# Second input split in groups of four blocks, ScalarE's dependent steps one product later, a fourth raw weight buffer

## The chip, the cores and the metric

The kernel runs on one core of one Trainium2 chip. The time is device microseconds of one execution; the median of three runs before the change is 1909.51 us (1908.23 to 1911.74). The engines are TensorE (PE; PEld are its weight loads), VectorE (DVE), ScalarE (ACT), GpSimd (POOL) and SyncE (SP), which issues the weight loads from memory.

## The reference

One step of a decoder layer on 264 tokens (256 of a prompt and 8 single ones), in fp32:

```python
h = h + 0.5 * swiglu(rmsnorm(h, g1), w1_gate, w1_up, w1_down)      # 2048 -> 5504 -> 2048
mix, states... = mixing_block(rmsnorm(h, gm), w_in, ...)           # mLSTM heads | gated convolution
h = h + mix
h = h + 0.5 * swiglu(rmsnorm(h, g2), w2_gate, w2_up, w2_down)
y = rmsnorm(h, g_final)

def swiglu(x, wg, wu, wd):
    return (jax.nn.silu(x @ wg) * (x @ wu)) @ wd
```

All weights are read once from memory (some 350 MB).

## The kernel before

**Split products.** Every fp32 operand is split into two fp16 parts: `high` (L249, ScalarE) rounds it, `low` (L257, VectorE) takes what is left. A product is the sum of high x high, high x low and low x high, so `three` (L384) issues three matmuls of 264 columns for each 128 x 128 block of weights. Activations lie transposed: 16 blocks of 128 channels x 264 tokens (`h[kb]`).

**Weights.** `plan` lists the weight tiles in the order of use. `fetch` (L263) takes the next: it issues its load on SyncE's queue (L284, L288, L292) into a raw fp32 buffer `wraw` of [128, 16, 128] (three of them), has ScalarE write the high part into `w` (four of them), and puts the low part into `held`; `release` (L327) issues VectorE's low part. About three products' tiles are under way ahead of TensorE (`room`, `AHEAD`). `wraw` comes free when its low part is done.

**Order of the work.** It is written out by hand. `tick` counts products (a half step in the middle of each), and `at(n, f)` issues `f` when the count is n further on. Each engine executes what was issued to it in order.

**A feed-forward layer** (`ffn`, L879) has two halves: gate and up products for 22 (21 in the second) blocks of 128 hidden channels, then 16 down products over these. A plain gate/up block `j` (`block`, L942) is two products of 48 matmuls; ScalarE takes the SiLU of the gate (L950, or L960 where the input is not yet scaled), VectorE multiplies by the up product (L899 or L897), and `activated` (L895) has ScalarE and VectorE split the result into `act[j]`.

**Pairs.** Blocks in `GU_SEVEN` (and some pairs of down blocks, `DOWN_SEVEN`) go through `product_pair` (L448): gate and up together, with high x high done plainly (L474) and the corrections by seven instead of eight block products on 132 columns each (L457, L458). For that VectorE forms sums of weights (`weight_sums`, L360 to L364) and sums of the input (`token_sums`, L446), and after it `join` (L503) puts the three banks together: a copy on ScalarE (L511), then `rest` on VectorE (L514 to L521). `by_seven` (L927) issues `rest` and, right behind it, ScalarE's SiLU (L933) one product later, and `activated` another half pair on.

**Second split of the input.** The first products of a layer run on the input without the norm's factor, since that factor `r` is not known yet; their results are multiplied by `r` (L957, L963). Meanwhile `renew` (L808) splits the input again, with gain and factor: for each of 16 blocks VectorE multiplies (L820), ScalarE takes the high part (`r`, L249), VectorE the low part (L257), two blocks every half product. `swap` makes the products use it from block 5 (first layer) or 3 (second) on; later `form` makes its token sums for the pairs.

**Range sums.** `watch` (L650) sums the absolute values of some columns of a result, on ScalarE (L658) in the feed-forward layers. The sums go into a test at the end of the kernel, on which a second pass in another number format depends. In a down product VectorE adds the result to `h` (L1020), and then the range sum of the same bank is issued.

**The mixing block** (`mix`, L1156) between the layers uses single buffers of the pool `tmp`, among them `wide` (L1359), which the tests use too.

Of the kernel before, what the change touches and what calls it, by code (L numbers as in the profile page):

```python
# [8 lines left out]
F32 = mybir.dt.float32  # L9
# [8 lines left out]
SEQ = 256  # L18
# [10 lines left out]
WK = 8  # L29
# [22 lines left out]
def spread(b0, b1, n):  # L52
# [1 line left out]


GU_SEVEN = {
    "1": spread(7, 21, 9) + spread(22, NFB - 1, 13), "2": spread(4, 21, 10) + spread(22, NFB - 1, 13),
}
DOWN_SEVEN = {
    ("1", 0): (1, 3, 4, 6, 7), ("1", 1): (1, 3, 4, 6),  # L60
# [112 lines left out]
def step(ctx: ExitStack, tc: tile.TileContext, a: dict, shared, bad=None):  # L173
# [89 lines left out]
    def fetch():  # L263

        if not plan:
            return
        key, src, n, m, several, sub = plan.pop(0)
        if half_size and key == "four":
            raw, parts = small()
        elif half_size and sub == 1:  # L270
            raw, parts = (t[:, WK:] for t in pair)
        elif half_size:
            raw = wpool.tile([128, WIDE, 128], F32, tag="wraw", name="wraw", bufs=3)
            parts = wpool.tile([128, WIDE, 2, 128], PART, tag="w", name="w", bufs=4)
# [25 lines left out]
        lows = []  # L300
        for src, h_, l_ in pairs:
            high(h_, src, sw)
            lows.append((l_, src, h_, sw))
        release()
        held.append((lows, (key, parts[:, :, 0], parts[:, :, 1], n, size(key, sub)), parts))
        if not lag[0]:
            release()


    held, lag, pair = [], [False], []  # L310

    def size(key, sub):
        return 0 if key == "four" else 2 if half_size and sub is None else 1
# [361 lines left out]

    def watch_tokens(z, j):

        sq = tmp.tile([128, 2, T], BF16, tag="yc", name="tokens", bufs=2)
        nc.scalar.activation(sq, z, AF.Square)

        def rest():
            ps = bank()[:, :T]
            for g in range(2):
                nc.tensor.matmul(ps, onesb, sq[:, g], start=(g == 0), stop=(g == 1))
            for i, op in enumerate((ALU.min, ALU.add)):
                nc.vector.tensor_reduce(
                    downs[:, i, j : j + 1], ps, axis=mybir.AxisListType.X, op=op
                )

        at(2, rest)  # L690
# [24 lines left out]
    def judge(x, bounds):  # L715

        n = x.shape[-1]
        ok = tmp.tile([128, 2 * SEQ], F32, tag="wide", name="ok", bufs=1)[:, :n]
        nc.vector.tensor_scalar(ok, x, bounds[0], None, op0=ALU.is_ge)
        nc.vector.scalar_tensor_tensor(  # L720
            ok, x, bounds[1], ok, op0=ALU.is_le, op1=ALU.mult
# [48 lines left out]
    class Norm:  # L770
# [34 lines left out]
            token_sums(t, self.groups[g])  # L805
            self.forms += [t[:, :, i] for i in range(4)]

        def renew(self, *blocks):  # L808

            for kb in blocks:  # L810
                g, i = kb // WK, kb % WK
                if kb == 0:
                    self.new = []
                if i == 0:
                    self.new.append(
                        self.fpool.tile([128, WK, 2, T], PART, tag=f"f{g}", name=f"r{g}")
                    )
                t, x = t264("sq"), self.new[g][:, i]
                gain = whole[:, self.col + kb : self.col + kb + 1]
                nc.vector.scalar_tensor_tensor(t, h[kb], gain, self.r, op0=ALU.mult, op1=ALU.mult)  # L820
                split(x, t, 1.0)

        def swap(self):
            self.groups, self.scaled = self.new, True
# [54 lines left out]
    def ffn(layer, norm, done, start=None, end=None):  # L879
        with ExitStack() as stack:  # L880
# [14 lines left out]
            def activated(j, i, zu, sg, src=None):  # L895
                if src is None:
                    nc.vector.tensor_tensor(zu, zu, sg, op=ALU.mult)  # L897
                else:
                    nc.vector.scalar_tensor_tensor(  # L899
                        zu, src, unit, sg, op0=ALU.mult, op1=ALU.mult  # L900
                    )
                g = i // WK
                if i % WK == 0:
                    groups[g] = apool.tile(
                        [128, min(WK, len(HALVES[0]) - i), 2, T], PART, tag=f"a{g}", name=f"a{g}"
                    )
                act[j] = t = groups[g][:, i % WK]
                high(t[:, 0, :], zu, sa[layer])
                rest = t[:, 1, :], zu, t[:, 0, :], sa[layer]
                if lag[0] and j < blocks[-1] - 2:  # L910
                    at(1.5, low, *rest)
                else:
                    low(*rest)
                n = len(blocks) // 2 * 2
                if half_size and i in (WK - 1, 2 * WK - 1, n - 1):
                    at(2, act_form, g, groups[g][:, : min(WK, n - WK * g)])

            groups, act_forms = {}, {}

# [6 lines left out]

            def by_seven(j, i):  # L927
                z, rest = join(product_pair((layer, "gu", j), norm.x, norm.forms, range(KB)))
                sg = t264("tb")

                def halves():
                    rest()
                    nc.scalar.activation(sg, z[:, 0], AF.Silu, scale=unit)  # L933

                at(1, halves)
                at(2, activated, j, i, z[:, 1], sg, z[:, 1])

            if half_size:
                spool[0] = stack.enter_context(tc.tile_pool(name=f"seven_{norm.tag}", bufs=1))
            for half, blocks in enumerate(HALVES):  # L940
                act = {}
                def block(i, j):  # L942
# [5 lines left out]
                    if norm.scaled:  # L948
                        sg = t264("tb")
                        nc.scalar.activation(sg, pg, AF.Silu, scale=unit)  # L950
                        watch(pg, scalar=True)
                        pu = gate_up(j, "u")
                        activated(j, i, t264("tc"), sg, pu)
                        watch(pu, scalar=True)
                        return
                    zg = t264("ta")
                    nc.vector.tensor_tensor(zg, pg, norm.r, op=ALU.mult)  # L957
                    watch(pg, scalar=True)
                    sg = t264("tb")
                    nc.scalar.activation(sg, zg, AF.Silu)  # L960
                    pu = gate_up(j, "u")
                    zu = t264("tc")
                    nc.vector.tensor_tensor(zu, pu, norm.r, op=ALU.mult)  # L963
                    activated(j, i, zu, sg)
                    watch(pu, scalar=True)

                for i, j in enumerate(blocks):
                    if half_size and j == (5 if start is not None else 3):
                        norm.swap()
                    if j in sevens:  # L970
                        by_seven(j, i)
# [6 lines left out]
                        for which in "gu":  # L978
                            early[2, which] = product((layer, which, 2), norm.x, range(KB))
                    if half_size and j == (3 if start is not None else 1):  # L980
                        for n in range(WK):
                            at(1 + n / 2, norm.renew, 2 * n, 2 * n + 1)
                        for g in range(2):
                            at(6 + g + (start is not None), norm.form, g)
                    lag[0] = half_size and j >= (3 if start is not None else 1)
                    if (j, "g") in early and not first:

# [17 lines left out]
                for db in range(0, KB - apart, 2):  # L1005
# [5 lines left out]
                    for i in (db, db + 1):  # L1011
                        final = half_size and i == KB - 1 and half == 1
                        if final:
# [3 lines left out]
                            (layer, "d", half, i), act, list(blocks),  # L1017
                            final=final,
                        )
                        nc.vector.scalar_tensor_tensor(  # L1020
                            h[i], ps, scale, h[i], op0=ALU.mult, op1=ALU.add
                        )
                        if half == 1:
                            done(i)
                        watch(ps, scalar=True)
                lag[0] = False
                release()
                if apart:
                    keys = [(layer, "d", half, db) for db in range(KB - apart, KB)]
                    end(keys, act, list(blocks), scale)  # L1030
# [90 lines left out]
    def judge_late():  # L1121

        late = stat[:, early[0] : len(stats)]
        n = len(stats) - early[0]
        ok = tmp.tile([128, 2, NSTAT], F32, tag="wide", name="ok", bufs=1)[:, :, :n]
        nc.vector.tensor_scalar(ok[:, 0], late, SUMS[0], None, op0=ALU.is_ge)
        count = const.tile([128, 1], F32, name="count")
        nc.vector.scalar_tensor_tensor(
# [27 lines left out]
def mix(tc, a, nm, n2, h, e):  # L1156
# [4 lines left out]
    product, split, rsqrt, column_sums, t264 = (  # L1161
        e["product"], e["split"], e["rsqrt"], e["column_sums"], e["t264"])
# [14 lines left out]
    for cb in range(8):  # L1177
        x3[8 + cb] = keep.tile([128, 2, T], PART, tag=f"yb{cb}", name=f"yb{cb}")
    ha = [keep.tile([128, 2, T], F32, tag=f"ha{i}", name=f"ha{i}") for i in range(NH)]

    inner = ExitStack()
    mp = inner.enter_context(tc.tile_pool(name="mixp", bufs=1))
# [125 lines left out]
    class Head:  # L1308
# [46 lines left out]

        def load_decays(self):
            if e["half_size"]:
                self.bc = tmp.tile([128, 2, SEQ], F32, tag="wide", name="bc", bufs=1)
            else:  # L1359
                self.bc = mp.tile([128, 2, SEQ], F32, tag="bc", name="bc", bufs=1)  # L1360
            queue.dma_start(self.bc, drows[self.hd].partition_broadcast(128))
# [480 lines left out]
```

## Time and profile before

| | |
|---|---|
| median of the runs | 1909.51 us |
| the profiled execution | 1917.14 us, its span 1915.4 us |
| mean granted TensorE clock | 0.978 |
| busy: TensorE / VectorE / ScalarE / GpSimd | 94% / 82% / 46% / 8% |
| read from memory | 366.72 MB, 198 GB/s with the writes over the span |

Rows of groups read: line, engine, operation, output<-inputs by the program's names, shapes, count | busy us, mean ns of one | idle time of the engine just before them and what ended it. Rows of waits: the engine, what it was to issue and its line <- whom it waited for: us in total, times, longest. Rows of the timeline: start us, duration us, engine, line, operation; in brackets the idle time before and what ended it. The granted clock is a share of full speed.

### The profile page before, as it was taken

Reading aid. Unit: us, or ns where it says so; the run is one execution under the profiler, and the core shown is the slowest. Engines: PE = TensorE matmul, PEld = TensorE weight load, DVE = VectorE, ACT = ScalarE, POOL = GpSimd, SP = SyncE. Lnnn points to the kernel's source line nnn. Section 1 sums busy time; section 2 is a strip of 40 time slices with the busy share of each in tenths; the row PEclk is TensorE's granted clock in tenths of the full one; section 3 lists DMA queues with packets and bytes.
Section 4 is the critical chain, followed back from the end, with each engine's and each line's share of the span. In section 5 each row is a group of like instructions: output and inputs, shape, how many; then the busy total and the mean of one; then the engine's idle time right before and its main releaser. Section 6 shows DMA issues by size and latency. Waiting matters only on the chain. (4 is left out here: it accounts for less than half of the span.)

```text
span 1915.4 us, 44686 instructions
## 1 busy us (share of the span) xinstructions
PE 1809.5 (94%) x19512; PEld 1605.0 (84%) x19512; DVE 1574.6 (82%) x2207; ACT 878.9 (46%) x1325; POOL 144.8 (8%) x200
## 2 busy tenths in 40 slices
PE   9699999999999989999999999799999999998996
PEld 7489889889898877888888888599989889897886
DVE  7688988898989788788888765789887898989775
ACT  7444443334344435376666644344443344443333
POOL 1000000000000122222120121000000000000021
PEclk9799999999999999999999999799999999999999
DMA  8255555565555556788886665365555565555543
GB/s 300 99 186 190 198 182 183 193 222 189 196 184 172 193 166 211 251 288 296 278 278 225 217 198 176 122 209 198 193 187 181 185 223 179 199 179 176 188 158 120
DMA packets 100684, 381.47 MB, mean 199 GB/s; under 512 B 10972, under 2 KB 20796, under 8 KB 90496
## 3 DMA queue, kind: packets, MB, share of 16 engines
q1 hardware_dynamic: 91280, 350.52, 54.4%
q0 software_dynamic: 8256, 27.57, 4.2%
q8 instruction: 154, 2.52, 0.5%
q10 hardware_dynamic: 944, 0.45, 0.1%
q14 instruction: 50, 0.41, 0.1%
HBM read 366.72 MB, written 11.78 MB: 198 GB/s over the span
## 5 line engine op out<-in xcount | busy, mean ns | idle before, releaser
L257 DVE SCALAR_TENSOR_TENSOR w<-wraw,w 128x2048 f16<-128x2048 f32 (+4 forms) x425 | 756.3, 1797 | 189.7 <-ACT w L249 189.4
L249 ACT ACTIVATE w<-wraw 128x2048 f16<-128x2048 f32 (+4 forms) x425 | 628.2, 1505 | 153.8 <-DMA wraw<-in_w1d 38.0
L387 PEld LDWEIGHTS <-w 128*128 128x128 f16 x3084 | 304.8, 99 | 110.7 <-DVE w L257 58.0
L386 PEld LDWEIGHTS <-w 128*128 128x128 f16 x3084 | 304.9, 99 | 75.6 <-issue 27.4
L385 PEld LDWEIGHTS <-w 128*128 128x128 f16 x3084 | 305.6, 99 | 51.9 <-ACT w L249 4.3
L387 PE MATMUL ps<-r,w 128*128 128x264 f16 x1056 | 299.3, 283 | 31.6 <-DVE w L257 31.6
L385 PE MATMUL ps<-r,w 128*128 128x264 f16 x1056 | 298.7, 283 | 23.3 <-ACT r L249 23.3
L386 PE MATMUL ps<-r,w 128*128 128x264 f16 x1056 | 298.4, 283 | 1.6 <-DVE r L257 0.2
L385 PE MATMUL ps<-xm,w 128*128 128x264 f16 x896 | 247.3, 276 | 0.0
L387 PE MATMUL ps<-xm,w 128*128 128x264 f16 x896 | 247.3, 276 | 0.0
L386 PE MATMUL ps<-xm,w 128*128 128x264 f16 x896 | 247.3, 276 | 0.0
L474 PEld LDWEIGHTS <-w 128*128 128x128 f16 x2174 | 208.3, 98 | 37.0 <-ACT w L249 8.2
L458 PEld LDWEIGHTS <-s 128*128 128x128 f16 x2160 | 209.6, 97 | 0.0
L457 PEld LDWEIGHTS <-s 128*128 128x128 f16 x2160 | 207.7, 96 | 0.5
L387 PE MATMUL ps<-a,w 128*128 128x264 f16 (+2 forms) x684 | 183.2, 274 | 17.2 <-DVE w L257 17.1
L385 PE MATMUL ps<-a,w 128*128 128x264 f16 (+2 forms) x684 | 183.3, 274 | 3.6 <-ACT w L249 3.6
L386 PE MATMUL ps<-a,w 128*128 128x264 f16 (+2 forms) x684 | 183.1, 273 | 0.0
L474 PE MATMUL ps<-r,w 128*128 128x264 f16 x1440 | 176.8, 276 | 3.4 <-ACT w L249 3.4
L360 DVE TENSOR_TENSOR s<-w 128x2048 f16<-128x2048 f16 (+1 forms) x141 | 166.3, 1180 | 7.5
L458 PEld LDWEIGHTS <-w 128*128 128x128 f16 x1634 | 159.2, 98 | 8.5 <-DVE w L257 6.4
L457 PEld LDWEIGHTS <-w 128*128 128x128 f16 x1634 | 159.1, 97 | 2.3
L457 PE MATMUL ps<-f,s 128*128 128x132 f16 x1080 | 133.7, 220 | 0.0
(284 smaller groups left out, 2657.5 us busy)
## 6 DMA issues: line engine op xcount, KB each, us to landing
wraw<-in_w2gu SPq DMA_DIRECT2D x86, 1024.0 KB, 5.1
wraw<-in_w1gu SPq DMA_DIRECT2D x82, 1024.0 KB, 5.4
wraw<-in_win SPq DMA_DIRECT2D x112, 512.0 KB, 5.7
wraw<-in_w1d SPq DMA_DIRECT2D x18, 1024.0 KB, 5.2
wraw<-in_wout SPq DMA_DIRECT2D x32, 512.0 KB, 4.8
wraw<-in_w2d SPq DMA_DIRECT2D x16, 1024.0 KB, 6.6
wraw<-in_w2d SPq DMA_DIRECT2D x22, 704.0 KB, 4.2
wraw<-in_w1d SPq DMA_DIRECT2D x20, 704.0 KB, 4.1
```

What stands on the lines that cost most here:

```text
L249: nc.scalar.activation(dst, src, AF.Copy, scale=scale)
L257: nc.vector.scalar_tensor_tensor(dst, src, scale, hi, op0=ALU.mult, op1=ALU.subtract)
L360: nc.vector.tensor_tensor(s[:, 0:2], bc, d_.unsqueeze(1).to_broadcast([128, 2, m, 2, 128]), op=ALU.add)
L385: nc.tensor.matmul(ps, wh, xk[:, 0, :], start=first, stop=False)
L386: nc.tensor.matmul(ps, wh, xk[:, 1, :], start=False, stop=False)
L387: nc.tensor.matmul(ps, wl, xk[:, 0, :], start=False, stop=last)
L457: nc.tensor.matmul(ps, w[0], x[:, 1], start=first, stop=False)
L458: nc.tensor.matmul(ps, w[1], x[:, 0], start=False, stop=last)
L474: nc.tensor.matmul(ps[:, :T], hi[:, i], xs[i][:, 0], start=(k0 + i == 0), stop=False)
```

## The change

- **Renewal.** `renew` takes four blocks in three steps half a product apart: VectorE's four products with gain and factor into an fp32 buffer `wide` (tag `g0`/`g1` of the layer's pool), one `high` over 4 x 264 elements on ScalarE, one subtraction over 4 x 264 on VectorE. The four groups start at 1, 1.5, 2.5 and 3 products. In the first layer the new input is used from block 6 on instead of 5, and the token sums come one step later.
- **ScalarE's steps.** In `by_seven` the SiLU is issued one tick behind `rest`, and the multiplication half a tick behind that. For all blocks on the renewed input but the last three of a half, `high` of the activation (`parted`) is issued one product after the multiplication, and its low part a product after that. The sums of activations for the down pairs start once a group is complete.
- **Range sums in front.** `watch` is issued before VectorE's reading of the same result.
- **A fourth raw buffer.** Every fourth tile of the feed-forward layers takes its `wraw` from the layer's own pool.
- **Fewer pairs.** Three gate/up blocks become plain: 8 and 12 in the first layer's halves (9 and 13 before), 10 and 12 in the second's (10 and 13).
- **Buffers.** `wide` of `tmp` goes: the tests use tag `ta`, the mixing block's `bc`, `zo`, `rs`, `yc` lie in its own pool.

```diff
-    "1": spread(7, 21, 9) + spread(22, NFB - 1, 13), "2": spread(4, 21, 10) + spread(22, NFB - 1, 13),
+    "1": spread(7, 21, 8) + spread(22, NFB - 1, 12), "2": spread(4, 21, 10) + spread(22, NFB - 1, 12),
...
+        elif half_size and spool[0] and key[0] in ("1", "2") and next(turn) % 4 == 3:
+            raw = spool[0].tile([128, WIDE, 128], F32, tag="wraw", name="wraw", bufs=1)
+            parts = wpool.tile([128, WIDE, 2, 128], PART, tag="w", name="w", bufs=4)
...
-        def renew(self, *blocks):
-            for kb in blocks:
...
-                t, x = t264("sq"), self.new[g][:, i]
-                gain = whole[:, self.col + kb : self.col + kb + 1]
-                nc.vector.scalar_tensor_tensor(t, h[kb], gain, self.r, op0=ALU.mult, op1=ALU.mult)
-                split(x, t, 1.0)
+        def renew(self, pool, k0, step):
+            g, i = k0 // WK, k0 % WK
+            if step == 0:
...
+                for k in range(4):
+                    gain = whole[:, self.col + k0 + k : self.col + k0 + k + 1]
+                    nc.vector.scalar_tensor_tensor(
+                        self.wide[g][:, i + k], h[k0 + k], gain, self.r, op0=ALU.mult,
+                        op1=ALU.mult,
+                    )
+                return
+            t, x = self.wide[g][:, i : i + 4], self.new[g][:, i : i + 4]
+            if step == 1:
+                high(x[:, :, 0], t, 1.0)
+            else:
+                nc.vector.tensor_tensor(x[:, :, 1], t, x[:, :, 0], op=ALU.subtract)
...
+                if src is None or j >= blocks[-1] - 2:
+                    parted(j, i, zu)
+                else:
+                    at(1.5, parted, j, i, zu)
+
+            def parted(j, i, zu):
...
                 high(t[:, 0, :], zu, sa[layer])
-                rest = t[:, 1, :], zu, t[:, 0, :], sa[layer]
+                rest = g, i, t[:, 1, :], zu, t[:, 0, :], sa[layer]
                 if lag[0] and j < blocks[-1] - 2:
-                    at(1.5, low, *rest)
+                    at(1.5, lower, *rest)
                 else:
-                    low(*rest)
+                    lower(*rest)
+
+            def lower(g, i, *rest):
+                low(*rest)
                 n = len(blocks) // 2 * 2
-                if half_size and i in (WK - 1, 2 * WK - 1, n - 1):
-                    at(2, act_form, g, groups[g][:, : min(WK, n - WK * g)])
+                count[g] += i < n
+                size = min(WK, n - WK * g)
+                if half_size and i < n and count[g] == size:
+                    at(1, act_form, g, groups[g][:, :size])
...
-                sg = t264("tb")
-                def halves():
-                    rest()
+                late = j >= blocks[-1] - 2
+                def gate():
+                    sg = t264("tb")
                     nc.scalar.activation(sg, z[:, 0], AF.Silu, scale=unit)
-                at(1, halves)
-                at(2, activated, j, i, z[:, 1], sg, z[:, 1])
+                    at(0.5, activated, j, i, z[:, 1], sg, z[:, 1])
+                at(1, rest)
+                at(1 if late else 2, gate)
...
                         pu = gate_up(j, "u")
+                        watch(pu, scalar=True)
                         activated(j, i, t264("tc"), sg, pu)
-                        watch(pu, scalar=True)
...
-                    if half_size and j == (5 if start is not None else 3):
+                    if half_size and j == (6 if start is not None else 3):
                         norm.swap()
...
-                        for n in range(WK):
-                            at(1 + n / 2, norm.renew, 2 * n, 2 * n + 1)
+                        for n, t in enumerate((1, 1.5, 2.5, 3)):
+                            for step in range(3):
+                                at(t + step / 2, norm.renew, spool[0], 4 * n, step)
                         for g in range(2):
-                            at(6 + g + (start is not None), norm.form, g)
+                            at(6 + g + 2 * (start is not None), norm.form, g)
...
+                        watch(ps, scalar=True)
                         nc.vector.scalar_tensor_tensor(
                             h[i], ps, scale, h[i], op0=ALU.mult, op1=ALU.add
                         )
                         if half == 1:
                             done(i)
-                        watch(ps, scalar=True)
...
-                self.bc = tmp.tile([128, 2, SEQ], F32, tag="wide", name="bc", bufs=1)
+                self.bc = keep.tile([128, 2, SEQ], F32, tag="bc", name="bc", bufs=1)
```

More of the change, by code (lines that the diff above doesn't have):

```diff
@@ L307, in fetch @@
             release()
-    held, lag, pair = [], [False], []
+    held, lag, pair, turn = [], [False], [], iter(range(10000))
     def size(key, sub):
@@ L676, in watch_tokens @@
     def watch_tokens(z, j):
-        sq = tmp.tile([128, 2, T], BF16, tag="yc", name="tokens", bufs=2)
+        sq = tmp.tile([128, 2, T], BF16, tag="ta", name="tokens", bufs=2)
         nc.scalar.activation(sq, z, AF.Square)
@@ L717, in judge @@
         n = x.shape[-1]
-        ok = tmp.tile([128, 2 * SEQ], F32, tag="wide", name="ok", bufs=1)[:, :n]
+        ok = t264("ta")[:, :n]
         nc.vector.tensor_scalar(ok, x, bounds[0], None, op0=ALU.is_ge)
@@ L806, in form @@
             self.forms += [t[:, :, i] for i in range(4)]
-        def renew(self, *blocks):
-            for kb in blocks:
-                g, i = kb // WK, kb % WK
-                if kb == 0:
-                    self.new = []
+        def renew(self, pool, k0, step):
+            g, i = k0 // WK, k0 % WK
+            if step == 0:
+                if k0 == 0:
+                    self.new, self.wide = [], []
                 if i == 0:
@@ L817, in renew @@
                     )
-                t, x = t264("sq"), self.new[g][:, i]
-                gain = whole[:, self.col + kb : self.col + kb + 1]
-                nc.vector.scalar_tensor_tensor(t, h[kb], gain, self.r, op0=ALU.mult, op1=ALU.mult)
-                split(x, t, 1.0)
+                    self.wide.append(
+                        pool.tile([128, WK, T], F32, tag=f"g{g}", name=f"t{g}")
+                    )
[4 more added lines that the diff above has]
+                        op1=ALU.mult,
+                    )
+                return
[4 more added lines that the diff above has]
+                nc.vector.tensor_tensor(x[:, :, 1], t, x[:, :, 0], op=ALU.subtract)
         def swap(self):
@@ L906, in activated @@
                     )
+                    count[g] = 0
                 act[j] = t = groups[g][:, i % WK]
                 high(t[:, 0, :], zu, sa[layer])
-                rest = t[:, 1, :], zu, t[:, 0, :], sa[layer]
+                rest = g, i, t[:, 1, :], zu, t[:, 0, :], sa[layer]
                 if lag[0] and j < blocks[-1] - 2:
-                    at(1.5, low, *rest)
+                    at(1.5, lower, *rest)
                 else:
-                    low(*rest)
+                    lower(*rest)
+            count = {}
+            def lower(g, i, *rest):
+                low(*rest)
                 n = len(blocks) // 2 * 2
-                if half_size and i in (WK - 1, 2 * WK - 1, n - 1):
-                    at(2, act_form, g, groups[g][:, : min(WK, n - WK * g)])
+                count[g] += i < n
+                size = min(WK, n - WK * g)
+                if half_size and i < n and count[g] == size:
+                    at(1, act_form, g, groups[g][:, :size])
             groups, act_forms = {}, {}
@@ L952, in block @@
                         pu = gate_up(j, "u")
+                        watch(pu, scalar=True)
                         activated(j, i, t264("tc"), sg, pu)
-                        watch(pu, scalar=True)
                         return
+                    watch(pg, scalar=True)
                     zg = t264("ta")
                     nc.vector.tensor_tensor(zg, pg, norm.r, op=ALU.mult)
-                    watch(pg, scalar=True)
                     sg = t264("tb")
@@ L961, in block @@
                     pu = gate_up(j, "u")
+                    watch(pu, scalar=True)
                     zu = t264("tc")
@@ L964, in block @@
                     activated(j, i, zu, sg)
-                    watch(pu, scalar=True)
                 for i, j in enumerate(blocks):
-                    if half_size and j == (5 if start is not None else 3):
+                    if half_size and j == (6 if start is not None else 3):
                         norm.swap()
@@ L1024, in ffn @@
                             done(i)
-                        watch(ps, scalar=True)
                 lag[0] = False
                 release()
+                if half:
+                    spool[0] = None
                 if apart:
@@ L1124, in judge_late @@
         n = len(stats) - early[0]
-        ok = tmp.tile([128, 2, NSTAT], F32, tag="wide", name="ok", bufs=1)[:, :, :n]
+        ok = t264("ta").rearrange("p (i n) -> p i n", i=2)[:, :, :n]
         nc.vector.tensor_scalar(ok[:, 0], late, SUMS[0], None, op0=ALU.is_ge)
@@ L1160, in mix @@
     ident, bg = e["ident"], e["bg"]
-    product, split, rsqrt, column_sums, t264 = (
-        e["product"], e["split"], e["rsqrt"], e["column_sums"], e["t264"])
+    product, split, rsqrt, column_sums = (
+        e["product"], e["split"], e["rsqrt"], e["column_sums"])
     bank, at, tick, queue, side = e["bank"], e["at"], e["tick"], e["queue"], e["side"]
@@ L1179, in mix, with t264 @@
     ha = [keep.tile([128, 2, T], F32, tag=f"ha{i}", name=f"ha{i}") for i in range(NH)]
+    def t264(tag, bufs=2, p=128):
+        pool = keep if tag in ("zo", "rs", "yc") else tmp
+        return pool.tile([p, T], F32, tag=tag, name=tag, bufs=bufs)
     inner = ExitStack()
```

## The prediction

> **What bounds the kernel now.** I read the page's busy shares and its clock slices first, then busy time by stretches of the span, then who waits for whom, then the groups by shape, and last single instructions at the places where TensorE stands still.
>
> ```profile
> PE 1809.5 (94%) x19512; PEld 1605.0 (84%) x19512; DVE 1574.6 (82%) x2207; ACT 878.9 (46%) x1325; POOL 144.8 (8%) x200
> PEclk9799999999999999999999999799999999999999
> ```
>
> TensorE is the bound over most of the span, so time can only be won where it idles or runs slowly. The clock digits fall to 7 twice, in slices 2 and 26. The stretches below (start:end, length, TensorE busy and matmul count, granted clock, DMA share, GB/s) cut the two feed-forward layers by stage.
>
> ```profile
> 63.50:107.50 44.00, 27.12 (x162) 0.69 0.37 123
> 1203.00:1237.30 34.30, 21.58 (x135) 0.70 0.38 129
> 115.00:300.00 185.00, 180.88 (x2175) 1.00 0.55 183
> 300.00:395.00 95.00, 89.26 (x1079) 0.98 0.58 193
> 395.00:600.00 205.00, 199.64 (x2438) 0.99 0.57 198
> 600.00:733.00 133.00, 120.42 (x1343) 0.99 0.54 173
> 1250.00:1440.00 190.00, 186.95 (x2152) 0.99 0.57 194
> 1440.00:1562.00 122.00, 114.38 (x1374) 0.97 0.58 197
> 1562.00:1765.00 203.00, 195.21 (x2427) 1.00 0.55 187
> 1765.00:1870.00 105.00, 97.37 (x1036) 0.97 0.54 177
> ```
>
> What each loses is idle time plus (1 - clock) x length. For the two renewals (first two rows) I count matmuls instead: a 264-column matmul starts every (1.96 - 0.28)/15 = 0.112 us (rows below), so 162 are worth 18.2 of 44.0 us and 135 worth 15.1 of 34.3: **lost 25.8 and 19.2 us**. The gate/up stages (rows 3, 5, 7, 9) lose 4.1 + 7.4 + 5.0 + 7.8 = **24 us**; the down stages of the first half of each layer (rows 4, 8) 7.6 + 11.3 = **19 us**; of the second half (rows 6, 10) 13.9 + 10.8 = **25 us**. All this is 113 us; the mixing block between keeps TensorE full.
>
> ```profile
> PE ps L387 <- DVE w L257: 50.7, 25, 4.7
> PE ps L385 <- ACT r L249: 23.3, 16, 3.2
> DVE w L257 <- ACT w L249: 189.4, 110, 3.9
> ACT tb L933 <- DVE y L519: 209.9, 45, 8.4
> ACT a L249 <- DVE tc L899: 146.8, 33, 8.3
> ACT a L249 <- DVE y L899: 97.3, 45, 6.2
> ACT seen L658 <- DVE h L1020: 80.0, 12, 8.0
> ACT xm L249 <- DVE h L1020: 44.9, 8, 7.7
> ACT w L249 <- DMA wraw<-in_w1d: 38.0, 13, 4.7
> ACT w L249 <- DMA wraw<-in_w2d: 35.3, 12, 4.7
> ```
>
> These rows (total, times, longest) name the loop. TensorE waits for the low parts of weights (VectorE, L257) and, in the renewals, for the renewed input's high parts (ScalarE, L249). VectorE in turn waits 189 us for ScalarE's high parts, and ScalarE is late because in its own queue it stands before something that VectorE has yet to produce: the SiLU of a pair, the high part of an activation, a range sum. A plain block shows it:
>
> ```profile
> 1247.35 0.42 ACT L249 ACTIVATE a<-tc 128x264 f16<-128x264 f32 x1 [5.76 <-DVE tc L899]
> 1247.84 3.70 ACT L249 ACTIVATE w<-wraw 128x2048 f16<-128x2048 f32 x2
> 1249.77 2.29 DVE L257 SCALAR_TENSOR_TENSOR w<-wraw,w 128x2048 f16<-128x2048 f32 x1 [2.45 <-ACT w L249]
> ```
>
> ScalarE idles 5.76 us until VectorE reaches `tc`; only then come two weight splits that could have run, and VectorE idles 2.45 us for the first.
>
> **The change, part by part.** Durations:
>
> ```profile
> L257 DVE SCALAR_TENSOR_TENSOR w<-wraw,w 128x2048 f16<-128x2048 f32 x202 | 461.6, 2287 | 132.2 <-ACT w L249 132.2
> L820 DVE SCALAR_TENSOR_TENSOR sq<-h,whole,rstd 128x264 f32<-128x264 f32 x32 | 15.6, 486 | 0.0
> L257 DVE SCALAR_TENSOR_TENSOR r<-sq,r 128x264 f16<-128x264 f32 x32 | 13.9, 433 | 26.5 <-ACT r L249 26.5
> L1594 DVE TENSOR_TENSOR jk<-cs,rb 128x1024 f32<-128x1024 f32 x16 | 19.5, 1218 | 0.0
> L446 DVE TENSOR_TENSOR g<-a 128x1056 f16<-128x1056 f16 x16 | 10.6, 703 | 0.1
> L249 ACT ACTIVATE w<-wraw 128x1024 f16<-128x1024 f32 x144 | 144.8, 1046 | 36.1 <-PE ps L387 14.4 <-DMA wraw<-in_win 9.1 <-PE ps L1280 6.4
> 49.69 0.48 DVE L820 SCALAR_TENSOR_TENSOR sq<-h,whole,rstd 128x264 f32<-128x264 f32 x1
> 1185.22 0.48 DVE L820 SCALAR_TENSOR_TENSOR sq<-h,whole,rstd 128x264 f32<-128x264 f32 x1
> 1200.19 0.28 PE L385 MATMUL ps<-r,w 128*128 128x264 f16 x1
> ```
>
> *Renewal four blocks at a time.* Before, a layer's renewal takes VectorE 16 x (0.486 + 0.433) = 14.7 us and 13.2 us of waiting for ScalarE. After: 16 x 0.486 = 7.8 us, and four low parts of 1056 elements. No row has that mix of fp32 and fp16 inputs; the bounds are 0.70 (1056 fp16) and 1.26 (1.218 x 1056/1024, fp32). I take 1.26, since one input is fp32: 12.8 us in all, with its ScalarE parts (1.046 x 1056/1024 = 1.08 us each) half a product or a product behind, so that VectorE finds them done. At the low bound 2.2 us more is won per layer.
>
> Layer 2: VectorE begins at 1185.2. Before the last four blocks are renewed its queue holds 12.8 us of renewal, three weight splits at 2.2 in succession and some 1.6 us of block 1: 1206.2. TensorE reaches the first new block at 1200.2 and the last four 12/16 of a 5.4 us product later, 1204.2. Late by 2 to 3 us, and such a gap can cost one spell of half clock, some 2 us: 4 of 19.2 remain, **-15**. Layer 1: the new input is first used one block later, at 63.5 + 2 x 5.4 = 74.3. From 49.7 VectorE has 12.8, three splits (6.6) and 6.6 of blocks 1 to 4, ending near 76; the split that block 5's up product needs is behind part of it, ready near 72 for a need at 69. Some 4 us of waiting and 2 of clock remain of 25.8: **-20**. Block 5 in the older form adds two 0.43 us products with `rstd` on VectorE, inside those 6.6. The range for both together is -24 to -42.
>
> Whether a short gap costs clock I take from the rows: in both renewals no single wait on `r` is over 3.2 us, yet the clock was 0.69 and 0.70. The Trainium skill ("TensorE: Matmul & The Clock Gate", Part 1) has the rate halved after at least one idle window of about 3.4 us; by that the remaining gaps would cost no clock and the sum would be 4 us lower. The trace disagrees where gaps follow each other closely.
>
> *ScalarE's steps one product later.* SiLU of a pair moves to half a pair after VectorE's joining, and high and low parts of an activation move one product behind their product on VectorE. No instruction is added. The waits on L933 and L899 (454 us of ScalarE's idle time) go wherever VectorE is less than a product (5 us) behind, and with them most of the 132 us that VectorE idles before 2048-wide splits. That alone is worth nothing off the path; on it are the 24 us of the gate/up stages. The last three blocks of each half keep the prompt order, and the waits at their ends (about 2 to 4 us in each of two second halves) stay. I take 9 us as left: **-15** (0 to -24). What is late next is the activation, by a product; its sums and the down products begin later than that. A pair's `y4` buffer is now let go only half a product before its turn comes again two pairs on, but the lists never have three pairs in a row.
>
> *Range sums in front, fourth raw buffer.* In the first halves' down stages ScalarE no longer stands before VectorE's `h` (80 us, up to 8.0); VectorE's `h` now stands behind the 0.17 us sum. The fourth buffer lets SyncE issue a load one split earlier, on the same queue, in the same order; that shortens the 73 us of waits for `w1d` and `w2d`. On the path are 19 us; I take half, **-10** (0 to -19). In the second halves ScalarE still waits for `h` at the next norm's split (L249 `xm`, 44.9), and the last stage for GpSimd's squares, so of 25 I take **-6** (from +5, if VectorE comes to wait for ScalarE there, to -25). The moved buffers of the mixing block keep their number: nothing.
>
> *Fewer pairs.* Counted from the lists, 45 pairs become 42.
>
> ```profile
> 1262.19 1.96 PE L474 MATMUL ps<-r,w 128*128 128x264 f16 x16
> 1267.21 1.96 PE L474 MATMUL ps<-r,w 128*128 128x264 f16 x16
> L360 DVE TENSOR_TENSOR s<-w 128x2048 f16<-128x2048 f16 x124 | 151.9, 1225 | 6.5
> L364 DVE TENSOR_TENSOR s<-s,w 128x1024 f16<-128x1024 f16 x124 | 85.8, 692 | 4.2
> ```
>
> Half a pair takes TensorE 5.02 us, so a pair 10.04; two plain products take 96 x 0.112 = 10.75. Three pairs less: **+2.2**. VectorE saves 2 x (1.225 + 2 x 0.692) = 5.2 us of sums for each, which is no gain of its own but lifts the cover of the gate/up stages.
>
> **Sum:** -20 - 15 - 15 - 10 - 6 + 2.2 = -64 us. The profiled execution took 1917.1 (span 1915.4, 1.7 around it), which would become 1853. It stands 7.6 over the median of the runs, 1909.5; taking the same difference from that gives **1846**.
>
> **Rivals.**
> *Only the renewals.* The gaps elsewhere come from VectorE's amount of work, not from its waits: 1909.5 - 35 + 2.2 = 1877. For it: at one of them VectorE had run without a break:
>
> ```profile
> 225.20 2.28 DVE L257 SCALAR_TENSOR_TENSOR w<-wraw,w 128x2048 f16<-128x2048 f32 x1
> 227.54 0.29 PE L387 MATMUL ps<-r,w 128*128 128x264 f16 x1 [2.66 <-DVE w L257]
> ```
>
> Against it: the backlog was built by the waits before, 132 us of them. Chance 0.2.
> *The renewal only half cured.* If the queue of splits behind the renewal is the limit, 15 of the 35 come back: 1866. Chance 0.1.
> *Nearly all gaps close:* 1909.5 - 35 - 24 - 19 - 25 + 2.2 = 1809. Against it, L249 `xm` and the prompt last blocks are untouched. Chance 0.1.
> *Slower.* In the down stages each `h` of VectorE now waits for a range sum, and that stands in ScalarE's queue behind weight splits waiting for DMA (73 us). If all of these pass through VectorE to TensorE, the down stages lose 73 instead of winning 16: 1909.5 - 35 - 15 + 2.2 + 73 = 1935. It decides from 48 us on, where it eats the rest. Against it: VectorE's next split needs that same high part anyway. Chance 0.05. The order itself is forced: the Trainium skill ("PSUM — Partial Sum Buffer", "PSUM bank collisions raise a hardware error") says that two engines must not be in one bank at once, reads against reads included; the 80 us row agrees, as range sum and `h` only share the bank that they read.
>
> **How the numbers follow.** My forecast has 0.55, on 1828 to 1864. The range adds the two rivals at 1866 and 1877, to 1880, and part of the way to 1809, to 1822; about 0.15 is outside. A measurement tells about 0.2% (4 us) from no change; every case but the last is well beyond it: faster 0.94, same 0.01, slower 0.05.
>
> **What would show it.** No wait of TensorE on `r`, clock digits 9 in slices 2 and 26; ScalarE's waits on L519 and L899 down from 454 us to under 100, VectorE's on weight splits from 189 to under 60; the second halves' down stages still losing over 15 us. I am wrong if TensorE's wait for low parts stays near 51 us with VectorE idle for ScalarE, or if VectorE appears waiting for range sums.

## The result, and the profile after

The changed kernel takes **1817.03 us** (median of 4 runs, 1816.34 to 1817.63) against 1909.68 us before: a ratio of 0.9514, 95% interval 0.9497 to 0.9530, 92.7 us less. The forecast was 1846 (1822 to 1880). The sign was right; the gain was half as large again as forecast, and the time lies 5 us below the range.

The page's busy shares and clock slices of the kernel after:

```profile
PE 1780.4 (98%) x19368; PEld 1596.7 (88%) x19368; DVE 1553.3 (86%) x2149; ACT 880.2 (49%) x1310; POOL 142.6 (8%) x200
PEclk9999999999999999999999999999999999999999
```

Both dips of the clock are gone. Next, TensorE by stage in both kernels (start:end, length, busy and matmul count, clock, DMA share, GB/s). The borders are the first matmul on activations (down stage) and the first on an input (gate/up stage). First before:

```profile
4.90:270.60 265.70, 241.54 (x2548) 0.95 0.56 192
270.60:388.90 118.30, 115.67 (x1390) 0.99 0.59 195
388.90:620.80 231.90, 219.66 (x2644) 0.99 0.56 192
620.80:743.30 122.50, 113.69 (x1256) 0.99 0.58 188
...
1167.30:1422.80 255.50, 239.65 (x2596) 0.95 0.53 177
1422.80:1540.90 118.10, 114.45 (x1391) 1.00 0.57 192
1540.90:1773.70 232.80, 221.04 (x2644) 0.99 0.57 192
1773.70:1915.40 141.70, 118.28 (x1340) 0.94 0.48 153
```

Then after, the same stages in the same order:

```profile
4.90:248.90 244.00, 235.62 (x2501) 0.99 0.63 218
248.90:362.70 113.80, 113.80 (x1391) 1.00 0.61 204
362.70:580.30 217.60, 217.60 (x2595) 1.00 0.61 204
580.30:695.40 115.10, 111.03 (x1253) 1.00 0.55 178
...
1118.00:1349.50 231.50, 230.81 (x2596) 1.00 0.60 202
1349.50:1463.30 113.80, 113.80 (x1390) 1.00 0.61 204
1463.30:1681.00 217.70, 217.70 (x2596) 1.00 0.61 204
1681.00:1814.60 133.60, 114.77 (x1340) 0.97 0.46 146
```

In four stages TensorE is busy over the whole length at full clock: what is left to win there is the matmul work itself, not gaps. The lengths fell, in order, by 21.7, 4.5, 14.3, 7.4, then 24.0, 4.3, 15.1 and 8.1 us, and the mixing block between by 1.4: 100.8 in all, the difference of the spans 1915.4 and 1814.6. (The profiled execution of before was 7.5 us above its median, that of after 0.7 below; hence 8 more than the medians differ by.)

Who waits for whom after (total, times, longest); ScalarE's old waits on VectorE have mostly become waits for TensorE:

```profile
PE ps L390 <- DVE w L257: 14.2, 10, 2.7
DVE w L257 <- ACT w L249: 120.3, 109, 3.4
ACT y L514 <- PE ps L461: 184.0, 50, 5.0
ACT seen L661 <- PE ps L390: 113.3, 47, 3.7
ACT a L249 <- DVE y L913: 67.9, 30, 7.1
ACT a L249 <- DVE tc L913: 27.2, 10, 6.4
ACT tb L961 <- DVE y L522: 24.2, 13, 4.7
DVE tc L913 <- ACT seen L661: 10.8, 8, 2.5
```

ScalarE now runs ahead until it needs a product that TensorE has not finished (L514, L661). Its waits for the joining and the products of VectorE fell from 454 us to 67.9 + 27.2 + 24.2 = 119. VectorE still waits 120 us for high parts, but TensorE waits 14 us for low parts instead of 51: most of that idling is not on TensorE's path.

### The profile page after: what moved, and what is told of

It is laid out like the page before. It is cut to its first block, busy times and chain, and to the rows that moved or that the text cites. A ratio compares the mean times of both kernels' runs of the same rounds, so it can differ in the third digit from the quotient of the medians.

```text
span 1814.6 us, 44307 instructions
## 1 busy us (share of the span) xinstructions
PE 1780.4 (98%) x19368; PEld 1596.7 (88%) x19368; DVE 1553.3 (86%) x2149; ACT 880.2 (49%) x1310; POOL 142.6 (8%) x200
## 4 chain that ended last, share of the span: by engine, by line
PE 79%; DVE 12%; ACT 3%; issue 3%; DMA 2%; POOL 1%; DVEq 0%; SPq 0%; ACTq 0%
PE ps L390 15%; PE ps L389 15%; PE ps L388 15%; PE ps L477 11%; PE ps L460 10%; PE ps L461 10%; DVE w L257 5%; ACT w L249 3%; DVE s L363 1%; DMA raw<-in_w1gu 1%; DVE s L366 1%; DVE t L826 1%; POOL sq L844 1%; DMA wraw<-in_w1gu 0%; DVE r L835 0%
## 5 line engine op out<-in xcount | busy, mean ns | idle before, releaser
L390 PE MATMUL ps<-r,w 128*128 128x264 f16 x1120 | 309.2, 276 | 1.3 <-DVE w L257 1.3
L389 PE MATMUL ps<-r,w 128*128 128x264 f16 x1120 | 309.2, 276 | 0.7 <-DVE r L835 0.7
L388 PE MATMUL ps<-r,w 128*128 128x264 f16 x1120 | 309.2, 276 | 0.0
L461 PEld LDWEIGHTS <-s 128*128 128x128 f16 x2064 | 200.3, 97 | 0.0
L460 PEld LDWEIGHTS <-s 128*128 128x128 f16 x2064 | 198.8, 96 | 0.1
L390 PE MATMUL ps<-a,w 128*128 128x264 f16 (+2 forms) x684 | 180.3, 269 | 8.5 <-DVE w L257 8.4
L388 PE MATMUL ps<-a,w 128*128 128x264 f16 (+2 forms) x684 | 180.3, 269 | 1.0 <-ACT w L249 1.0
L389 PE MATMUL ps<-a,w 128*128 128x264 f16 (+2 forms) x684 | 180.3, 269 | 0.0
L363 DVE TENSOR_TENSOR s<-w 128x2048 f16<-128x2048 f16 (+2 forms) x135 | 159.0, 1178 | 7.3 <-DVE w L257 0.5
L477 PE MATMUL ps<-r,w 128*128 128x264 f16 x1344 | 164.9, 276 | 0.0
L460 PE MATMUL ps<-f,s 128*128 128x132 f16 x1008 | 124.8, 220 | 0.0
```

Of the source, the lines that this page charges most:

```text
L363: nc.vector.tensor_tensor(s[:, 0:2], bc, d_.unsqueeze(1).to_broadcast([128, 2, m, 2, 128]), op=ALU.add)
L388: nc.tensor.matmul(ps, wh, xk[:, 0, :], start=first, stop=False)
L389: nc.tensor.matmul(ps, wh, xk[:, 1, :], start=False, stop=False)
L390: nc.tensor.matmul(ps, wl, xk[:, 0, :], start=False, stop=last)
L460: nc.tensor.matmul(ps, w[0], x[:, 1], start=first, stop=False)
L461: nc.tensor.matmul(ps, w[1], x[:, 0], start=False, stop=last)
```

## The experiments

Three theories stood at first. A: the gate/up losses came from ScalarE standing in its queue before VectorE's results, and the late steps cured them. B: the fourth raw buffer let both engines run ahead. C: VectorE's amount of work was at its limit, and three pairs less eased it. Each kernel differs from one of the two by the edit shown. In "x over", the other kernel is the one after (1817.03).

**1. Late steps undone.**

```diff
-                at(1, rest)
-                at(1 if late else 2, gate)
+                at(1, halves)                 # rest(), then SiLU
+                at(2, activated, j, i, z[:, 1], sg, z[:, 1])
...
-                    at(1.5, parted, j, i, zu)   # high and low parts a product later
```

> The kernel after with ScalarE's steps as prompt as before (SiLU of a pair right behind VectorE's joining, high and low part of an activation right behind the product); all else as after. Theory A (ScalarE's queue standing before VectorE caused the gate/up losses, and the late steps cured them): 25 to 38 us come back, 1842 to 1855, with the gaps in the four gate/up stages. Theory B (the fourth raw buffer lets both engines run ahead, whatever the order): under 10 us, 1817 to 1827. Theory C (VectorE's amount of work, eased by three pairs less): under 10 us.

Measured: 1832.60 us, 15.6 over; ratio to before 0.9601 (0.9585 to 0.9617). Between what theories A and C expected: the late steps matter, but they do not carry all that the gate/up stages lost. The stages lengthen at other places than theory A said: the first halves' gate/up stages to 250.0 and 238.0 us (from 244.0 and 231.5), those of the second halves only to 218.8 each (from 217.6 and 217.7).

**2. Three raw buffers.**

```diff
-        elif half_size and spool[0] and key[0] in ("1", "2") and next(turn) % 4 == 3:
-            raw = spool[0].tile([128, WIDE, 128], F32, tag="wraw", name="wraw", bufs=1)
...                                            # and the lines that serve this buffer
```

> The kernel after with three raw weight buffers instead of four. Theory A: at most 8 us come back, mostly in the down stages, 1817 to 1825, with waits of ScalarE for DMA back in the profile. Theory B: 20 to 40 us come back, 1837 to 1857, in gate/up and down stages alike.

Measured: 1818.83 us, 1.8 over. Theory B falls. The profile of this run has ScalarE waiting for `w1d` again,

```profile
ACT w L249 <- DMA wraw<-in_w1d: 23.1, 10, 4.5
```

a wait that is absent from the profile after, and it costs next to nothing.

**3. Range sums behind again.**

```diff
-                        watch(pu, scalar=True)
                         activated(j, i, t264("tc"), sg, pu)
+                        watch(pu, scalar=True)
...                                            # the same in the other plain blocks and the down products
```

> The kernel after with the range sums behind VectorE's reading of the same bank, as before. Theory A says that ScalarE then stands before VectorE again in the down stages: 5 to 12 us come back, 1822 to 1829, with the wait of the range sum for h back at some 80 us. Theory B and C: under 4 us.

Measured: 1858.69 us, **41.7 over**; ratio to before 0.9738 (0.9722 to 0.9754). No theory had this. Its waits, its gate/up stage of the first layer's second half, and one sum in ScalarE's queue there (a sum is two rows) with what follows:

```profile
ACT seen L661 <- DVE tc L913: 271.1, 31, 10.6
ACT seen L661 <- DVE h L1050: 81.7, 12, 7.9
```
```profile
371.60:595.30 223.70, 218.60 (x2596) 1.00 0.58 193
```

```profile
413.14 0.18 ACT L661 ACTIVATE seen<-ps 128x16 f32<-128x16 f32 x1 [10.27 <-DVE tc L913]
413.22 0.19 ACT L661 ACTIVATION_READ_ACCUMULATOR seen<-ps 128x1 f32 x1
413.31 1.90 ACT L249 ACTIVATE w<-wraw 128x2048 f16<-128x2048 f32 x1
```

The sum takes 0.18 us, but it reads the bank that VectorE's product reads, and as that was issued first the sum waits for it: 10.3 us here, with a weight split right behind it. In the kernel before, the high part of the activation stood in the same place and took the blame (`ACT a <- DVE tc`, 146.8 us); the sum came right behind it and had nothing left to wait for, as in the plain block that the prediction shows:

```profile
1247.68 0.17 ACT L658 ACTIVATE seen<-ps 128x16 f32<-128x16 f32 x1
```

With the high part moved away, the range sum inherits the wait.

**4. The old renewal.**

```diff
-                        for n, t in enumerate((1, 1.5, 2.5, 3)):
-                            for step in range(3):
-                                at(t + step / 2, norm.renew, spool[0], 4 * n, step)
+                        for n in range(WK):
+                            at(1 + n / 2, norm.renew, 2 * n, 2 * n + 1)
...                                            # the old body of renew; new input from block 5, its sums a step earlier
```

> The kernel after with the renewal two blocks at a time and its new input used from block 5 on, as before. All theories: the two renewals cost 30 to 45 us again, 1847 to 1862, and the clock falls to half there; below 1840 if the fourth buffer and the late steps by themselves took part of it away.

Measured: 1850.73 us, 33.7 over, within what all expected.

After these four, theory Q: what counts is the order in ScalarE's queue, range sums included.

**5. The longer lists, on the kernel after.**

```diff
-    "1": spread(7, 21, 8) + spread(22, NFB - 1, 12), "2": spread(4, 21, 10) + spread(22, NFB - 1, 12),
+    "1": spread(7, 21, 9) + spread(22, NFB - 1, 13), "2": spread(4, 21, 10) + spread(22, NFB - 1, 13),
```

> The kernel after with the longer lists of before (45 gate/up pairs instead of 42). Theory Q (what stalled the gate/up stages was the order in ScalarE's queue, so VectorE now has room for three pairs more): TensorE saves 3 x 0.7 us, 1814 to 1816. Theory C (VectorE's amount of work was at its limit and the shorter lists were needed): 1820 or more, with TensorE waiting for low parts again.

Measured: 1815.12 us, ratio to before 0.9508 (0.9495 to 0.9521), as Q expected; the interval does not separate it from the kernel after (0.9497 to 0.9530). The stage of the first layer's second half, again busy throughout, takes 216.9 us instead of 217.6:

```profile
361.50:578.40 216.90, 216.90 (x2642) 1.00 0.61 205
```

**6. Late steps alone, on the kernel before** (edit 1 the other way round).

> The kernel before with ScalarE's late steps alone. Theory Q (in a plain block the range sum, which must wait for VectorE's reading of the same bank, is then what ScalarE stands before, so the late steps need the range sums in front): 1902 to 1912, with ScalarE's wait for the product on VectorE now at the range sum. Theory A (the late steps act by themselves): 1875 to 1895.

Measured: 1905.95 us against 1908.66 in the same runs; ratio 0.9983 (0.9973 to 0.9992). As Q says: the wait has moved to the range sum, and next to nothing is won.

```profile
ACT seen L658 <- DVE tc L899: 243.7, 29, 10.6
```

**7. Range sums in front alone, on the kernel before** (edit 3 the other way round).

> The kernel before with the range sums in front alone. Theory Q: the down stages win 10 to 16 us, the gate/up stages little, since ScalarE still stands before VectorE with the high part of the activation: 1893 to 1902. Theory A (range sums matter only in the down stages of the first halves, 19 us at most): 1895 to 1905. The part won in the gate/up stages tells them apart.

Measured: 1879.46 us; ratio 0.9842 (0.9827 to 0.9857), 29.2 less, more than either reading expected. The gate/up stage of the first layer's second half, and one wait:

```profile
383.80:609.00 225.20, 218.10 (x2643) 1.00 0.58 195
```
```profile
ACT a L249 <- DVE tc L899: 125.7, 33, 4.9
```

That stage has 225.2 us instead of 231.9, although ScalarE still stands before VectorE's `tc` with the high part, now for 4.9 us at most instead of 8.3. I had expected little there. Much of it is won at the border to the stage ahead: the first matmul on the first pair's token sums starts 13.5 us into the stage, against 16.8 before (second layer: 13.5 against 20.5), so 3.3 of the 6.7 us and 7.0 of the 7.0 us that these two stages win are won before it, right behind the down products. Both first halves' down stages take 113.8 us here, busy throughout, against 118.3 and 118.1. The range sums of the down products alone were not put in front on the kernel before, so how much of the 29.2 us is theirs is not shown.

**8. The new renewal alone, on the kernel before** (edit 4 the other way round).

> The kernel before with the renewal four blocks at a time alone (new input from block 6 on in the first layer). If the renewal's gain stands by itself: 30 to 40 us less, 1870 to 1880, and no half clock at the renewals. If it needs the other parts (ScalarE free of waits, so that its high parts come in time): 1880 to 1900.

Measured: 1887.22 us; ratio 0.9887 (0.9872 to 0.9902), 21.4 less: the second case. But not for the reason given there, as its stretches show (the renewals and what follows them in the same stage):

```profile
63.50:107.50 44.00, 40.39 (x380) 1.00 0.50 168
107.50:261.70 154.20, 143.49 (x1704) 0.98 0.55 184
1191.00:1225.30 34.30, 31.71 (x336) 1.00 0.49 162
1225.30:1396.90 171.60, 166.30 (x1948) 0.98 0.57 194
```

The renewals lose only 3.6 and 2.6 us. The rest of the stages now loses 10.7 + 3.1 and 5.3 + 3.4 us; in the kernel before these rests were

```profile
107.50:270.60 163.10, 158.98 (x1905) 1.00 0.55 186
1237.30:1422.80 185.50, 182.45 (x2150) 0.99 0.56 189
```

4.1 and 4.9 us. Some 39 us are won at the renewals and 13 given back: TensorE comes to the pairs earlier, while VectorE is held up by ScalarE as before (`DVE w <- ACT w` 188.3 us, 189.4 before).

**9. Sums in front in the plain blocks only** (edit 3 for the down products alone).

> The kernel after with the range sums in front in the plain gate/up blocks only; in the down products they stand behind VectorE's addition to h again. If each place costs its own stage: 12 to 20 us over the kernel after, 1829 to 1837, lost in the down stages, gate/up stages as after. If the late result of the down stages is carried into the gate/up stages behind them: over 1840.

Measured: 1824.95 us, 7.9 over, less than the first case's 1829 to 1837. Its place is that of the second case in good part. ScalarE's waits for `h` are back in full (80.0 us in 12 waits, all in the two first halves' down stages), yet these stages have no gap:

```profile
249.00:362.80 113.80, 113.80 (x1390) 1.00 0.58 196
```

The gate/up stages behind them take 219.7 and 222.2 us instead of 217.6 and 217.7, and all of that is lost before the first matmul on token sums (15.5 and 18.0 us into the stage instead of 13.5 in both). The second halves' down stages take 117.2 and 135.2 us instead of 115.1 and 133.6. By difference, with the late steps in place, the plain blocks carry about 34 of edit 3's 41.7 us.

**10. Sums behind, but on VectorE.**

```diff
-                        watch(pu, scalar=True)
                         activated(j, i, t264("tc"), sg, pu)
+                        watch(pu)                # a VectorE reduction of 16 columns
...                                            # the same at the other places of edit 3
```

> The kernel after with all these range sums behind again, but done on VectorE (0.165 us each), so that no engine waits for another's reading of the bank. If it is ScalarE's wait for VectorE at the shared bank that cost 42 us: 1817 to 1824, since some 120 sums add 20 us of work to a VectorE that is 86% busy. If what counted was that the bank or the result came free later: 1845 to 1860.

Measured: 1814.59 us; ratio 0.9517 (0.9502 to 0.9532), no different from the kernel after. The place behind is harmless once no engine waits for another's reading; 81 of the sums went over (the SiLU's own banks keep theirs on ScalarE), 13 us of work that VectorE had room for.

```profile
L665 DVE TENSOR_REDUCE stat<-ps 128x1 f32<-128x16 f32 x155 | 25.3, 163 | 0.0
```

**11. Late steps and sums in front together, on the kernel before.**

> The kernel before with the late steps and the range sums in front together (old renewal, three raw buffers, old lists). If the two only add: 1909 - 2.7 - 29.2, 1875 to 1880. If the late steps need the sums in front: 1850 to 1868, with the second halves' gate/up stages near 217 us each.

Measured: 1850.77 us; ratio 0.9709 (0.9694 to 0.9725), **56.4 less** than the 1907.16 beside it, where the two alone give 2.7 and 29.2. This is with three raw buffers and 45 pairs. Four of its stages: the first layer's first down stage, second half's gate/up stage and second down stage, and the last down stage:

```profile
265.50:379.30 113.80, 113.80 (x1390) 1.00 0.60 198
379.30:596.20 216.90, 216.90 (x2644) 1.00 0.61 207
596.20:712.80 116.60, 111.06 (x1253) 1.00 0.56 183
1713.70:1847.70 134.00, 114.98 (x1340) 0.97 0.48 153
```

The first two are without a gap.

**12. 48 pairs.**

```diff
-    "1": spread(7, 21, 8) + spread(22, NFB - 1, 12), "2": spread(4, 21, 10) + spread(22, NFB - 1, 12),
+    "1": spread(7, 21, 9) + spread(22, NFB - 1, 14), "2": spread(4, 21, 11) + spread(22, NFB - 1, 14),
```

> The kernel after with 48 gate/up pairs (9 and 14 in the first layer's halves, 11 and 14 in the second's) instead of 42. If VectorE still keeps up: 6 x 0.7 us less, 1812 to 1814. If its amount of work becomes the limit (14 pairs are some 210 us of VectorE in a stage of 216): 1817 to 1830, with TensorE waiting for low parts.

Measured: 1813.60 us (1812.97 to 1814.01); ratio 0.9510 (0.9498 to 0.9523). VectorE still keeps up: both second halves' gate/up stages take 216 us and have no gap. The median is 3.4 us under the kernel after, but the intervals overlap, so "better" is not shown.

## Why the prediction was wrong

*Renewal: right.* Forecast -35. The two renewals lost 45 us before, counted by matmuls; after, by idle time and clock, the stretch 63.5 to 107.5 loses 5.4 and the one that answers to the second 0.7, so 39 were won. The time from a stage's first matmul to its first one on token sums, the same work in both kernels, says the same: 119.6 and 76.7 us before, 99.6 and 58.2 after. Experiment 4, the renewal undone alone, gives 33.7.

```profile
63.50:107.50 44.00, 40.36 (x369) 0.96 0.49 168
1153.50:1187.80 34.30, 33.61 (x353) 1.00 0.58 192
```

The queue worked out by hand came true for the first layer almost to the microsecond: the last low part was to end near 76, the split for block 5's up product to be ready near 72.

```profile
70.93 2.29 DVE L257 SCALAR_TENSOR_TENSOR w<-wraw,w 128x2048 f16<-128x2048 f32 x1 [0.67 <-ACT w L249]
73.28 0.39 PE L390 MATMUL ps<-x,w 128*128 128x264 f16 x1 [1.93 <-DVE w L257]
75.33 1.25 DVE L835 TENSOR_TENSOR r<-t,r 128x1056 f16<-128x1056 f32 x1
```

The split ended at 73.2 and the last low part at 76.6; the 1056-element subtraction took 1.25 us, the bound I had taken. In the second layer the 4 us that I had counted as staying shrank to the 0.7. What the term left out is experiment 8: alone, a third of it would have been given back.

*Fewer pairs: right.* +2.2 forecast; a stage with one pair less takes 0.7 us longer (217.6 against 216.9), so some 2 us for three. They were not needed either: with 45 and 48 pairs the second halves' gate/up stages have no gap.

*Down stages of the first halves: right in size by luck, wrong in cause.* They became 8.8 us shorter (4.5 + 4.3) against 10. But I halved a loss of 19 us that my rows overstated: between the true borders it was 2.6 + 1.2 and 3.7 us, and all of it went. The fourth buffer, which I counted there, is not needed: with three buffers the stage takes the same 113.8 us (experiment 11). Nor was ScalarE's 80 us of waiting for `h` what these stages lost by: in experiment 9 it is all back and they still take 113.8 us; it costs some us in the stages behind.

*Gate/up stages: the step that failed.* "I take 9 us as left: -15" stands against 36 us: the four stages became 75.1 us shorter, 38.9 of them at the renewals. Two errors of size make it up. First, the loss was put at 24 us because my stretches had round borders: the starts and the ends of both second halves lay in rows that I counted as down stages. Cut at the true borders, the second halves alone lost 12.2 + 2.3 and 11.8 + 2.3 us of idle time and clock, and with the 4.1 and 4.9 us behind the renewals (rows of experiment 8) it is 38. Second, the discount. I kept 9 us, of which the prompt last blocks explained 4 to 8, and no row priced these; after, under 1 us is left in three of these stages, and 1.7 us of idle time in the fourth behind its renewal.

*The cause was in the wrong line.* I priced the range sums in the down products only, put them at nothing in the plain blocks, and wrote that there "ScalarE idles 5.76 us until VectorE reaches `tc`" because of the high part. The sum stood right behind that high part, on the same bank, and would have waited as long. The late steps win 2.7 us alone (experiment 6) and the sums 29.2 (experiment 7), but both together 56.4 (experiment 11): the late steps need the sums in front. Experiment 9 puts about 34 of the sums' 41.7 us in the plain blocks. Undone one at a time on the kernel after, the edits cost 33.7 us for the renewal (forecast 35), 15.6 for the late steps (forecast 15), and 41.7 for the sums with 1.8 for the buffer (forecast 10 + 6). So by edits, too, the term that was mis-sized is that of the range sums. That the late steps come out at their forecast is in part chance: I had put their gain on the losses of all four gate/up stages, more than half of them in the second halves, and undoing them costs the first halves most (experiment 1).

*Down stages of the second halves: mis-sized as well.* -6 forecast, 7.4 + 8.1 = 15.5 measured. My last row ended at 1870, 45 us before the end; between the true borders these stages lost 8.8 + 1.2 and 23.4 + 8.5 us, not 25 in all. The waits that I named as staying did stay (`ACT xm <- DVE h` 37.3 and 19.4 us after, 44.9 and 9.8 before), and yet the stages became shorter. Experiment 11 has them at 116.6 and 134.0 us against 115.1 and 133.6, so nearly all of it is again the freed queue. Most of that is the range sums: in front alone (experiment 7) they bring the stages to 118.6 and 137.5 us, while the late steps alone (experiment 6) leave them at 120.7 and 141.6.

*The rivals.* "Nearly all gaps close" (1809, chance 0.1) came nearest, 8 us off, but not term by term: it closed 25 us in the second halves' down stages, of which 15.5 came, and 24 in the gate/up stages, where 36 came. "Only the renewals" argued that VectorE's amount of work is the limit; experiments 5 and 12 contradict it: more work for VectorE, no gaps. "The renewal only half cured" does not fit the 39 us; its 1866 was also a slip, since 1846 + 15 is 1861. "Slower" named a wait of VectorE for range sums; it exists, 10.8 us in 8 waits on `tc` at L913 and 3.8 us in the blocks that are not yet scaled, but none on `h`.

*The signs.* The clock digits and TensorE's wait on `r` came as said (0.7 us left), and the second halves' down stages still lose 27 us. Two sizes were missed although more was won than forecast: ScalarE's waits fell to 119 us, not under 100, and VectorE's on weight splits to 120, not under 60. How long an engine waits in total did not tell what its waits cost.

*Half clock after short gaps:* in the stretch from 63.5 the clock still loses (1 - 0.96) x 44 = 1.8 us, of the 2 that I had counted. The gaps there:

```profile
64.56 0.29 PE L390 MATMUL ps<-x,w 128*128 128x264 f16 x1 [0.67 <-DVE w L257]
70.95 0.29 PE L388 MATMUL ps<-x,w 128*128 128x264 f16 x1 [1.04 <-ACT w L249]
```

With the one of 1.93 us above they are all far under the idle window of 3.4 us that the Trainium skill names ("TensorE: Matmul & The Clock Gate", Part 1), so trace and page differ here too. Such gaps do not cost clock each time: in experiment 5 the same three and one of 1.21 us stand in this stretch, and its clock is 1.00. Of the prediction's two renewals only the second, with no gap over 3.2 us, bears on this; in the first I looked only at the waits on `r` and passed over one for a low part, which is longer than the page's window:

```profile
68.54 0.40 PE L387 MATMUL ps<-r,w 128*128 128x264 f16 x1 [4.75 <-DVE w L257]
```

## What to carry to other kernels

When two engines wait for each other, list everything that one of them has in its queue between the wait that the profile names and the work that is wanted: the next instruction with the same dependence inherits the wait, and moving only the named one won 2.7 us here. Count a stage's loss between its true borders, up to the end of the span, and leave part of it uncured only for a wait that has its own row. A gap closed in front of an engine that is still held up can be partly given back further on, so closing several together can be worth more than the sum of each alone (here 56.4 us against 2.7 + 29.2).

## What the runs showed of the hardware

81 range sums of 0.18 us on ScalarE cost 42 us of the whole by their place in the queue alone; the same 81 in that place but on VectorE (0.163 us each) cost nothing that could be measured. That two engines may not read one bank at once was not tried; what the runs show is the wait in the program's order and its price.
